# Two transformer blocks in one program: the small products of two pairs of recurrent heads and of the attention heads in common steps, between runs of 21 dense products

## The chip, the cores and the metric

One core of a Trainium2 chip runs the whole program in one launch. The metric is device time in microseconds (us), the median of several runs. A profile of one execution stands beside the times.

The engines: TensorE (PE in the profile; its weight loads are PEld) multiplies, VectorE (DVE) and ScalarE (ACT) do the elementwise work, GpSimd (POOL) a little of it, SyncE (SP) issues the weight transfers. Each engine executes its own list in order and waits where a value that it needs isn't there.

## The reference, cut to what matters

256 tokens of width 2048 (and 16 learned tokens ahead of them in the first block), float32. The first block computes, from one input projection, 16 recurrent heads (RWKV-7), 16 attention heads with a forget gate, and gates that merge the two:

```python
xn = _rms(h, n1)
z_rwkv, z_fox, z_gate = jnp.split(xn @ w_in, ...)
y_a = _rwkv7(z_rwkv + (z_prev - z_rwkv) * mu, ...)   # 16 heads of 64
y_b = _fox(z_fox, ...)                               # 16 heads of 64
merged = g_a * (y_a @ w_a) + g_b * (y_b @ w_b)
h = h + merged @ w_o
h = h + (jax.nn.silu(gate) * up) @ w_dn              # gate, up = _rms(h, n2) @ w_gu

def step(S, inp):                                    # in _rwkv7, per token
    r_t, w_t, k_t, v_t, a_t, b_t = inp               # a = -kk, b = kk * a
    sa = jnp.einsum('bhvk,bhk->bhv', S, a_t)
    S = S * w_t[:, :, None, :] + sa[..., None] * b_t[:, :, None, :] + v_t[..., None] * k_t[:, :, None, :]
    return S, jnp.einsum('bhvk,bhk->bhv', S, r_t)
```

kk is k normalised over the 64 values of a head; the heads' outputs are normalised per head, and a bonus term sum(r * k * r_k) * v is added. In _fox q and k are normalised per head and the scores carry the sums of the log forget gates. The second block has a Hyena convolution, latent attention (MLA) and a gated feed-forward with a short convolution; its filters come from a small network with two sines.

## The kernel before, in words

Activations lie feature-major, 128 features by tokens. A dense product takes a weight block of 128x128 float32 (a "k step"), split into a high part (wh, a cast on ScalarE, line 192) and a low part (wl, a subtraction on VectorE, line 193), and three matmuls for it: wh with the high part of x, wl with the high part, wh with the low part (`mm3`, lines 216 to 218). Weights come in pieces of 8 k steps, that is 24 matmuls, through three buffers each for the raw piece wr, for wh and for wl. PSUM has four tags of two buffers: d for the dense products of the heads' stage, and a, b, c for the small ones.

The stage of the heads (`phase_heads`) is 80 dense blocks of 16 k steps, in the order of `in_order`: for each of 8 pairs of recurrent heads the blocks k, v, r; for each pair of attention heads fk, fq, fv; and 32 gate blocks, which `GATES_PER_PAIR` spreads among the pairs. In between come the small products. For a recurrent pair (`rwkv_pair`) these are, one behind the other: a first headsum (sums over each head's 64 rows, `headsum`, lines 296 and 297: a product with the block matrix bo of a high part rs_r and a low part rs_q) for the norm of kk; on VectorE then a, b and the bonus term; a second headsum for that term; matrices within chunks of 64 tokens (gs, psum a); four levels of an inverse (lines 1228 and 1232); transposes; the recurrence over five chunks (psum c); and the group norm with two more headsums. `rstd` is 1/sqrt from ScalarE with a correction on VectorE (lines 313 to 322). `fox_pair` has a headsum each for k and q (`headnorm`), then scores, softmax, transposes and values for each head.

The code of a pair is written in one piece. The framework's scheduler decides by priorities (the order of the code, with weights ahead) and due times where each instruction goes on its engine; so the small products fall among the dense ones singly or in groups.

Behind the heads: the merge, w_o, the first feed-forward; then the mix (`phase_mix`), beside which `filters` works out the Hyena filters (its sines on ScalarE, L747; `transforms` loads fspec and splits it into dh and dl); `phase_out`, whose `rstd` has a "warm" argument: products without use, written by PE in the time of the norm; the convolution feed-forward; and `phase_last`, with w_down2.

Of the kernel before, what the change touches and what calls it, by code (L numbers as in the profile page):

```python
# [18 lines left out]
P = 128  # L19
# [35 lines left out]
GATES_PER_PAIR = (2, 0, 2, 3, 3, 2, 2, 2, 0)  # L55
# [96 lines left out]
class Builder:  # L152
# [60 lines left out]
    def mm3(self, out, wh, wl, xh, xl, start, stop):  # L213

        nc = self.nc
        nc.tensor.matmul(out, lhsT=wh, rhs=xh, start=start, stop=False)  # L216
        nc.tensor.matmul(out, lhsT=wl, rhs=xh, start=False, stop=False)  # L217
        nc.tensor.matmul(out, lhsT=wh, rhs=xl, start=False, stop=stop)  # L218
# [71 lines left out]
    def headsum(self, ps, w, src, n, pool=None):  # L290

        hi, lo = (self.tl(pool or self.small, [P, L if pool is None else n], t)[:, :n] for t in ("rs_r", "rs_q"))
        hi = hi.bitcast(F32R)
        lo = lo.bitcast(F32R)
        self.split(src, hi, lo)
        self.nc.tensor.matmul(ps, lhsT=w, rhs=hi, start=True, stop=False)
        self.nc.tensor.matmul(ps, lhsT=w, rhs=lo, start=False, stop=True)

# [5 lines left out]
    def rstd(self, out, ss, n, scale, eps, floor=None, pool=None, warm=None):  # L304
# [13 lines left out]
        for x in (r, q) if warm is not None else ():  # L318

            nc.tensor.matmul(warm, lhsT=self.con("ones"), rhs=x, start=True, stop=True)  # L320
# [4 lines left out]
    def run(self):  # L325
# [8 lines left out]
        self.wlo = self.pool(ctx, "wlo", 3)  # L334
        self.psum = {t: self.pool(ctx, "ps" + t, 2, PSUM) for t in "dabc"}
# [120 lines left out]
    def fox_pair(self, j):  # L456
        nc, w, w2 = self.nc, self.pfx, self.pfx2
        ident = self.con("ident")
        kn = self.headnorm(self.proj("fk", j, 0), 0, w, w2, "fk", self.col("kg"))
        qn = self.headnorm(self.proj("fq", j, NM), NM, w, w2, "fq", self.qgs)  # L460
        ps = self.proj("fv", j, 0)
        v = self.tl(w, [P, T], "fv")
        nc.vector.tensor_tensor(out=v, in0=ps, in1=self.R, op=ALU.mult)
        vt = self.tl(w2, [P, 3, P], "fvt")
# [6 lines left out]
        y = self.tl(w2, [P, S], "fy")  # L471
        for h in range(2):
            hs = slice(64 * h, 64 * h + 64)
            sel = self.oh[hs, 2 * j + h : 2 * j + h + 1].broadcast_to([64, P])
            pt = self.tl(w, [P, 5, P], "fpt")
            for b in range(2):
# [8 lines left out]
                self.softmax(sc, mx, -1.0, w2)  # L485
                ps = self.ps("b").rearrange("p (c x) -> p c x", c=4)
# [9 lines left out]
            out = self.ps("b")[:, :S]  # L496
            nc.tensor.matmul(out[hs], lhsT=vt[:, 0, hs], rhs=pt[:, 0:2], start=True, stop=False)
            nc.tensor.matmul(out[hs, 0:128], lhsT=vt[:16, 1, hs], rhs=pt[:16, 3], start=False, stop=False)
            nc.tensor.matmul(out[hs, 128:256], lhsT=vt[:, 1, hs], rhs=pt[:, 2], start=False, stop=False)
            nc.tensor.matmul(out[hs, 128:256], lhsT=vt[:16, 2, hs], rhs=pt[:16, 4], start=False, stop=True)  # L500
            nc.scalar.copy(y[hs], out[hs])
        nc.scalar.dma_start(out=self.sp_yb[j], in_=y)

    def headnorm(self, ps, t0, w, w2, tag, gain):
# [7 lines left out]
        ps = self.ps("b")[:, :n]  # L512
        self.headsum(ps, self.bo, sq, n, w)
# [3 lines left out]
        return zn  # L517
# [79 lines left out]
    def phase_mix(self, xh, xl, ys, rs):  # L597
# [3 lines left out]
        with ExitStack() as c:  # L601
# [24 lines left out]
            accq, rq, acck = (self.tl(w, [P, S], n) for n in ("rope_t", "rq", "acch"))  # L626
            cqh, cql = (self.tl(w, [P, 4, S], n, F32R) for n in ("hyh", "hyl"))
# [11 lines left out]
            self.rstd(acck, self.total(acck), S, 1.0 / 256, 1e-6)  # L639
            kvh, kvl = (self.tl(w, [P, 2, S], n, F32R) for n in ("huh", "hul"))  # L640
# [76 lines left out]
    def filters(self, c):  # L717
# [5 lines left out]
        dh, dl = (self.tl(w, [P, 1024], n, F32R) for n in ("dh", "dl"))  # L723
        cfi = self.tl(w, [P, S], "cfi")
# [7 lines left out]
        self.transforms(w, ((dh, dl, 0),))  # L732
        dh, dl = (x.rearrange("p (k f) -> p k f", k=2) for x in (dh, dl))
# [23 lines left out]
        h2 = sine(ps, self.col("f_b2"), self.col("f_f2"), "s2")  # L757
        yield
# [169 lines left out]
    def phase_last(self, pg, hh, hl, spill):  # L928
# [20 lines left out]
        for g in range(4):  # L949
            gs = slice(512 * g, 512 * g + 512)  # L950
            ps = [self.ps("a"), self.ps("d")]
            for i in range(HT // 2):
                wh, wl = (x.rearrange("p (k x) c -> p k (x c)", k=2) for x in self.weights(a["w_down2"][22 * g + i], PIECE))
# [83 lines left out]
    def phase_heads(self):  # L1037
# [5 lines left out]
        with ExitStack() as pr:  # L1043
# [39 lines left out]
            self.fox_setup(pr)  # L1083
            for j in range(9):
                if j < 8:
                    self.rwkv_pair(j, w)
                if j == 0:
                    self.forget_gates()
                if j:
                    self.fox_pair(j - 1)  # L1090
                for _ in range(GATES_PER_PAIR[j]):
                    self.gate()
            while self.ngate < 32:
                self.gate()

# [19 lines left out]
    def rwkv_pair(self, j, w):  # L1115
# [8 lines left out]
        self.lerp(self.proj("r", j, 14), self.col("mu_r", j), 14, 16, zr[:, 64:])  # L1124

# [20 lines left out]
        nc.vector.scalar_tensor_tensor(out=kk, in0=z, scalar=self.col("k_k", j), in1=kk, op0=ALU.mult, op1=ALU.mult)  # L1146
        bk = self.tl(w, [P, NC5, 2, 64], "bk")
# [13 lines left out]
        ps = self.ps("b")[:, :S]  # L1161
        self.headsum(ps, self.bo, t1[:, 64:], S)
# [6 lines left out]
        gm = self.crw("gmask").rearrange("p (x t) -> p x t", x=2)  # L1169
        for h in range(2):  # L1170
            hs = slice(64 * h, 64 * h + 64)
# [9 lines left out]

        uv = self.tl(w2, [P, NC5, P], "uv")
        v0 = self.tl(w2, [64, NC5, 64], "v0")
        bt = self.tl(w2, [P, NC5, P], "bt")
        bs = self.tl(w, [P, NC5, P], "bs")
        ed = self.tl(w2, [P, NC5], "ed")
        nc.gpsimd.tensor_copy(ed, ee[:, 0].rearrange("p (c t) -> p c t", t=64)[:, :, 63])
        for c in range(NC5 - 1):
            nc.vector.tensor_scalar(out=bs[:, c], in0=bk[:, c].rearrange("p x t -> p (x t)"),
                                    scalar1=ed[:, c : c + 1], scalar2=None, op0=ALU.mult)  # L1190
# [4 lines left out]
        for c0, n in ((0, 3), (3, 2)):  # L1195
            ps = self.ps("a").rearrange("p (c x) -> p c x", c=4)
            for c in range(n):
                nc.tensor.transpose(ps[:, c], zv[:, 64 * (c0 + c) : 64 * (c0 + c) + 128], self.con("ident"))
            nc.scalar.copy(uv[64:128, c0 : c0 + n], ps[64:128, :n])
            nc.vector.tensor_copy(v0[:, c0 : c0 + n], ps[64:128, :n, 0:64])  # L1200
# [17 lines left out]
        for lv in range(1, 5):  # L1218
# [3 lines left out]
            lm = level(lv, c0)  # L1222
            ps = pv()
# [4 lines left out]
            nc.vector.tensor_tensor(out=pp[:, c0:], in0=ps[:, c0:], in1=eye.broadcast_to([P, n, 64]), op=ALU.add)  # L1228
            ps = pv()
# [10 lines left out]
            if lv == 3:  # L1240
                nc.gpsimd.tensor_copy(xf[:, 0], xt[:, 0])
        ps = self.ps("a")[:, :P].rearrange("p (c t) -> p c t", c=4)
# [6 lines left out]
        nc.scalar.copy(y5[96:128], ps[96:128])  # L1249
# [186 lines left out]
```

## Time and profile before

| what | us |
|---|---|
| median of 3 runs (lowest, highest) | 2824.17 (2823.87, 2826.2) |
| the profiled execution | 2825.54 |
| its span | 2823.8 |
| PE busy in the span | 2798.4 |
| heads' stage, 31.4 to 785.9 | 754.5, PE busy 753.81 |
| the rest, 785.9 to the end | 2037.9, PE busy 2015.81 |
| VectorE, ScalarE busy in the heads' stage | 518.7, 411.3 |

How to read it: a row of the timeline has start and length in us, engine, line, operation, the tiles written and read, the shape of the array's use (rows*columns) and of the operands. In square brackets stands the idle time in front and what ended it. Starts of neighbours on PE lie closer than the lengths say, since matmuls are pipelined. The granted clock is 1.00 at full speed.

### The profile page before, as it was taken

How to read it: one execution, taken by the hardware profiler on the slowest of the kernel's cores; microseconds unless marked ns; L12 is line 12 of the kernel's file. 1: busy time of each engine (PE TensorE's matmuls, PEld its weight loads, DVE VectorE, ACT ScalarE, POOL GpSimd, SP SyncE). 2: the span in 40 equal slices, each digit the busy share in tenths (PEclk: the TensorE clock that was granted, in tenths of full speed). 3: DMA queues.
4: the chain of work that ended last, by engine and by line, in shares of the span. 5: the costliest groups of instructions: out<-in, count | busy, mean ns of one | idle time of the engine just before them, and what ended most of it. 6: DMA issues, size and time to landing. Idle time of an engine off the chain costs nothing.

```text
span 2823.8 us, 56202 instructions
## 1 busy us (share of the span) xinstructions
PE 2798.4 (99%) x23288; PEld 2637.9 (93%) x23288; DVE 1847.1 (65%) x2958; ACT 1346.8 (48%) x1994; POOL 143.2 (5%) x294
## 2 busy tenths in 40 slices
PE   9999999999999999999999999999999999999998
PEld 9988888888999999999999999999989999998886
DVE  8857667676566665656565556787787777775444
ACT  7545555555444554444444445444454444444443
POOL 0000000010000200000000000001100000000000
PEclk9999999999999999999999999999999999999999
DMA  7333333334576555566656666444556555556554
GB/s 246 128 110 116 102 109 116 106 105 137 184 238 211 189 188 195 194 194 194 194 195 201 202 202 216 162 148 144 189 192 193 194 194 194 194 193 230 191 191 163
DMA packets 147741, 497.13 MB, mean 176 GB/s; under 512 B 16252, under 2 KB 30941, under 8 KB 146909
## 3 DMA queue, kind: packets, MB, share of 16 engines
q1 hardware_dynamic: 128448, 458.42, 49.7%
q10 hardware_dynamic: 18396, 33.03, 3.4%
q8 instruction: 182, 2.98, 0.4%
q0 software_dynamic: 640, 2.10, 0.3%
q14 instruction: 75, 0.61, 0.1%
HBM read 478.27 MB, written 15.20 MB: 175 GB/s over the span
## 4 chain that ended last, share of the span: by engine, by line
PE 96%; DVE 2%; DMA 1%; ACT 1%; issue 0%; POOL 0%; DVEq 0%; ACTq 0%; POOLq 0%
PE psd L218 12%; PE psd L216 12%; PE psd L217 12%; PE psa L217 5%; PE psa L218 5%; PE psb L218 5%; PE psb L216 5%; PE psa L216 5%; PE psb L217 5%; PE psc L217 4%; PE psc L218 4%; PE psc L216 4%; PE psa L959 1%; PE psd L960 1%; PE psa L960 1%; PE psd L959 1%
## 5 line engine op out<-in xcount | busy, mean ns | idle before, releaser
L193 DVE TENSOR_TENSOR wl<-wr,wh 128x1024 fp32r<-128x1024 f32 (+1 forms) x872 | 1063.7, 1220 | 629.1 <-ACT wh L192 627.9
L192 ACT CAST wh<-wr 128x1024 fp32r<-128x1024 f32 (+1 forms) x872 | 909.1, 1043 | 1157.6 <-PE psd L218 337.4
L218 PE MATMUL psd<-xl,wh 128*128 128x256 f32 (+2 forms) x1280 | 370.4, 289 | 0.0
L216 PE MATMUL psd<-xh,wh 128*128 128x256 f32 (+2 forms) x1280 | 369.5, 289 | 0.0
L217 PE MATMUL psd<-xh,wl 128*128 128x256 f32 (+2 forms) x1280 | 367.9, 287 | 0.4 <-DVE wl L193 0.4
L218 PEld LDWEIGHTS psd<-xl,wh 128*128 128x128 f32 x1280 | 240.6, 188 | 7.7 <-issue 2.3
L217 PEld LDWEIGHTS psd<-xh,wl 128*128 128x128 f32 x1280 | 240.8, 188 | 6.5 <-issue 2.1
L216 PEld LDWEIGHTS psd<-xh,wh 128*128 128x128 f32 x1280 | 240.6, 188 | 6.3 <-issue 1.8
L218 PE MATMUL psd<-x3l,wh 128*128 128x256 f32 x496 | 140.7, 284 | 0.0
L216 PE MATMUL psd<-x3h,wh 128*128 128x256 f32 x496 | 140.6, 283 | 0.0
L217 PE MATMUL psd<-x3h,wl 128*128 128x256 f32 x496 | 138.9, 280 | 0.0
L216 PE MATMUL psd<-x4h,wh 128*128 128x256 f32 x368 | 100.5, 277 | 2.8 <-ACT x4h L252 2.8
L217 PE MATMUL psd<-x4h,wl 128*128 128x256 f32 x368 | 101.5, 277 | 1.1 <-DVE wl L193 1.0
L218 PE MATMUL psd<-x4l,wh 128*128 128x256 f32 x368 | 101.2, 277 | 0.0
L262 POOL TENSOR_TENSOR acc<-acc,ssq 128x256 f32<-128x256 f32 x42 | 58.4, 1391 | 817.8 <-ACT ssq L264 813.4
L217 PE MATMUL psa<-x4h,wl 128*128 128x256 f32 x352 | 97.0, 277 | 1.0 <-DVE wl L193 1.0
L218 PE MATMUL psa<-x2l,wh 128*128 128x256 f32 x352 | 97.4, 277 | 0.0
L216 PE MATMUL psa<-x2h,wh 128*128 128x256 f32 x352 | 97.4, 277 | 0.0
L218 PE MATMUL psb<-x2l,wh 128*128 128x256 f32 x352 | 97.2, 276 | 0.0
L217 PE MATMUL psb<-x2h,wl 128*128 128x256 f32 x352 | 97.2, 276 | 0.0
L216 PE MATMUL psb<-x2h,wh 128*128 128x256 f32 x352 | 97.2, 276 | 0.0
L218 PE MATMUL psc<-x2l,wh 128*128 128x256 f32 x352 | 97.2, 276 | 0.0
(673 smaller groups left out, 8390.9 us busy)
## 6 DMA issues: line engine op xcount, KB each, us to landing
wr<-w_in_dram SPq DMA_DIRECT2D x230, 512.0 KB, 3.4
wr<-w_gu_dram SPq DMA_DIRECT2D x176, 512.0 KB, 4.1
wr<-w_down_dram SPq DMA_DIRECT2D x176, 512.0 KB, 4.2
wr<-w_up_dram SPq DMA_DIRECT2D x176, 512.0 KB, 3.5
wr<-w_ab_dram SPq DMA_DIRECT2D x32, 512.0 KB, 4.2
wr<-w_o_dram SPq DMA_DIRECT2D x32, 512.0 KB, 3.4
wr<-w_out_dram SPq DMA_DIRECT2D x32, 512.0 KB, 3.6
spill_g<-acc ACTq DMA_DIRECT2D x32, 128.0 KB, 2.1
```

The costliest lines, as they stand in the source:

```text
L192: self.nc.scalar.copy(hi, src)
L193: self.nc.vector.tensor_tensor(out=lo, in0=src, in1=hi.bitcast(F32), op=ALU.subtract)
L216: nc.tensor.matmul(out, lhsT=wh, rhs=xh, start=start, stop=False)
L217: nc.tensor.matmul(out, lhsT=wl, rhs=xh, start=False, stop=False)
L218: nc.tensor.matmul(out, lhsT=wh, rhs=xl, start=False, stop=stop)
L262: nc.gpsimd.tensor_tensor(out=acc, in0=acc, in1=self.pending[id(acc)], op=ALU.add)
L959: nc.tensor.matmul(ps[b], lhsT=hh[:, k, bs], rhs=wl[:, q], start=False, stop=False)
L960: nc.tensor.matmul(ps[b], lhsT=hl[:, k, bs], rhs=wh[:, q], start=False, stop=k == HT - 1)
```

## The change: what it does

`rwkv_pair`, `headnorm`, `headsum` and the attention heads become generators ("chains") that stop at marked places (`yield`). `dense` counts its k steps. After every 7 of them (TICK, 21 matmuls) every chain that is alive goes one step on, that is, it issues what lies between two marks. The step's instructions are ordered behind the dense product before it, and the next dense product behind the step's instructions on PE. Up to two recurrent pairs and a pair of attention heads are alive at a time.

Along with that: the blocks k, v, r and their shifts are in `rwkv_inputs`; the transposes of v stand between the first two headsums; the products k-v of all five chunks are made in one group before the recurrence, which then adds them on VectorE; the values of the attention heads take psum a, and both score blocks of a head are in one step, with their transposes two steps later; `GATES_PER_PAIR` is new, and the forget gates are worked out within the first pair's gate blocks.

Outside the heads: `transforms` stands behind the second sine in `filters`; the warm products in `rstd` are six in place of two; three pads (48, 32 and 16 columns) move tiles in `phase_mix` and `filters`; the weights of w_down2 lie 48 columns further in their buffers.

```diff
-GATES_PER_PAIR = (2, 0, 2, 3, 3, 2, 2, 2, 0)
+GATES_PER_PAIR = (5, 2, 3, 2, 3, 2, 3, 5, 0)
+TICK = 7
...
     def dense(self, out, st, kt, xh, xl, tok):
         for k in range(kt):
             wh, wl = next(st)
-            self.mm3(out, wh, wl, xh[:, k, tok], xl[:, k, tok], k == 0, k == kt - 1)
+            with ExitStack() as held:
+                for i in self.hold:
+                    held.enter_context(self.tc.issue_after(i))
+                m = self.mm3(out, wh, wl, xh[:, k, tok], xl[:, k, tok], k == 0, k == kt - 1).ins
+            self.hold = []
+            self.since += 1
+            if self.chains:
+                self.hold = [m]
+                if self.since >= TICK:
+                    self.since = 0
+                    self.tick(m)
+
+    def tick(self, ins):
+        for c in list(self.chains):
+            with self.tc.issue_after(ins):
+                if next(c, self) is self:
+                    self.chains.remove(c)
+        traced = self.nc.cur_bb.bb.instructions
+        at = next(k for k in reversed(range(len(traced))) if traced[k] is ins)
+        self.hold = [i for i in traced[at:] if i.engine == ins.engine]
...
-    def headsum(self, ps, w, src, n, pool=None):
+    def headsum(self, bank, w, src, n, pool=None):
...
         self.split(src, hi, lo)
+        yield
+        ps = self.ps(bank)[:, :n]
         self.nc.tensor.matmul(ps, lhsT=w, rhs=hi, start=True, stop=False)
         self.nc.tensor.matmul(ps, lhsT=w, rhs=lo, start=False, stop=True)
+        return ps
...
-        for x in (r, q) if warm is not None else ():
+        for x in (r, r, r, q, q, q) if warm is not None else ():
...
-        self.transforms(w, ((dh, dl, 0),))
...
         h2 = sine(ps, self.col("f_b2"), self.col("f_f2"), "s2")
+        self.transforms(w, ((dh, dl, 0),))
...
+            self.tl(w, [P, 48], "apart")
...
+            self.tl(w, [P, 32], "away")
...
-                wh, wl = (... for x in self.weights(a["w_down2"][22 * g + i], PIECE))
+                wh, wl = (... for x in self.weights(a["w_down2"][22 * g + i], PIECE, off=48))
...
             for j in range(9):
                 if j < 8:
-                    self.rwkv_pair(j, w)
-                if j == 0:
-                    self.forget_gates()
+                    self.rwkv_inputs(j)
+                    self.drain(pairs[-2:-1])
+                    pairs.append(self.chain(self.rwkv_pair(j, w)))
                 if j:
-                    self.fox_pair(j - 1)
-                for _ in range(GATES_PER_PAIR[j]):
+                    self.drain(fox)
+                    fox = [self.fox_pair(j - 1)]
+                else:
+                    fox = []
+                for i in range(GATES_PER_PAIR[j]):
                     self.gate()
+                    if i == 1 and j == 0:
+                        self.forget_gates()
...
     def rwkv_pair(self, j, w):
...
-        ps = self.ps("b")[:, :L]
-        self.headsum(ps, self.bo, sq, L)
+        ps = yield from self.headsum("b", self.bo, sq, L)
         kk = self.tl(w, [P, L], "kk")
         self.rstd(kk, ps, L, 1.0, 0.0, floor=1e-24)
         nc.vector.scalar_tensor_tensor(out=kk, in0=z, ...)
+        yield
+        for c0, n in ((0, 3), (3, 2)):
+            ps = self.ps("a").rearrange("p (c x) -> p c x", c=4)
+            for c in range(n):
+                nc.tensor.transpose(ps[:, c], zv[:, ...], self.con("ident"))
...
-        ps = self.ps("b")[:, :S]
-        self.headsum(ps, self.bo, t1[:, 64:], S)
+        ps = yield from self.headsum("b", self.bo, t1[:, 64:], S)
...
+        for c in range(NC5):
+            for h, hs in enumerate(hss):
+                kat, vv = ...
+                nc.tensor.matmul(ps[hs, c], lhsT=kat, rhs=vv, start=True, stop=True)
+        kv = v0
+        nc.scalar.copy(kv, ps)
```

Where this puts instructions, at three places. New line numbers are higher: the dense matmuls are L217 to L219, the headsum L333 and L334, the splits L194 on VectorE. Names carry buffer numbers.

On PE, the first headsum of the first pair. Before, its two products stand apart, behind several hundred dense rows of the opening:

```order
L217 MATMUL psd_237_1268<-xh_6_94,wl_240_1271 128x272
L218 MATMUL psd_237_1268<-xl_7_95,wh_239_1270 128x272
L296 MATMUL psb_115_735<-rs_r_116_736,bo_67_472 128x320
L216 MATMUL psd_237_1268<-xh_6_94,wh_239_1270 128x272
L217 MATMUL psd_237_1268<-xh_6_94,wl_240_1271 128x272
...
L218 MATMUL psd_237_1268<-xl_7_95,wh_242_1300 128x272
L297 MATMUL psb_115_735<-rs_q_117_737,bo_67_472 128x320
L216 MATMUL psd_237_1268<-xh_6_94,wh_242_1300 128x272
```

After, both stand in one step, three rows behind the products of the gate of the recurrence (psb with adh and adl):

```order
L217 MATMUL psd_117_739<-xh_6_94,wh_119_741 128x256
L218 MATMUL psd_117_739<-xh_6_94,wl_120_742 128x256
L219 MATMUL psd_117_739<-xl_7_95,wh_119_741 128x256
L217 MATMUL psb_110_720<-adh_56_447,wh_107_709 128x272
L218 MATMUL psb_110_720<-adh_56_447,wl_108_710 128x272
L219 MATMUL psb_110_720<-adl_57_448,wh_107_709 128x272
L333 MATMUL psb_121_749<-rs_r_115_735,bo_67_472 128x320
L334 MATMUL psb_121_749<-rs_q_116_736,bo_67_472 128x320
L217 MATMUL psd_117_739<-xh_6_94,wh_119_741 128x256
```

The headsum moved forward on PE by some hundred dense rows.

On PE, the second headsum of the second pair (pair 1). Before, it is together with a headsum of the attention's keys (the one of 272 columns):

```order
L218 MATMUL psd_409_2045<-xl_7_95,wh_414_2077 128x272
L1232 MATMUL psa_153_850<-xt_146_828,pp_152_848 64x64 x10
L296 MATMUL psb_284_1524<-rs_r_285_1525,bo_67_472 128x256
L297 MATMUL psb_284_1524<-rs_q_286_1526,bo_67_472 128x256
L296 MATMUL psb_386_1946<-rs_r_387_1947,bo_67_472 128x272
L297 MATMUL psb_386_1946<-rs_q_388_1948,bo_67_472 128x272
L216 MATMUL psd_409_2045<-xh_6_94,wh_414_2077 128x272
```

After, products of the first pair's recurrence (psc) stand in the same step:

```order
L219 MATMUL psd_289_1693<-xl_7_95,wh_291_1695 128x256
L1371 MATMUL psc_294_1713<-st_276_1647,ar_131_797 64x64 x2
...
L1360 MATMUL psc_295_1717<-ar_131_797,st_241_1499 64x64
L333 MATMUL psb_296_1723<-rs_r_283_1672,bo_67_472 128x256
L333 MATMUL psb_305_1740<-rs_r_287_1689,bo_67_472 128x272
L334 MATMUL psb_305_1740<-rs_q_288_1690,bo_67_472 128x272
L334 MATMUL psb_296_1723<-rs_q_284_1673,bo_67_472 128x256
L217 MATMUL psd_289_1693<-xh_6_94,wh_291_1695 128x256
```

Between the pair's first headsum and this one there are 42 dense rows now.

On VectorE, the end of the work for that headsum (kk to the split rs_q of the bonus term t). Before:

```order
L1154 TENSOR_SCALAR t1_282_1514<-av_53_442,cols_1_61 128x320
L193 TENSOR_TENSOR wl_415_2078<-wr_413_2076,wh_414_2077 128x8x128
L1155 SCALAR_TENSOR_TENSOR kf_283_1515<-t1_282_1514,kz1_49_435 128x320
L509 TENSOR_TENSOR fq_400_2024<-psd_393_1963,R_3_85 128x256
L193 TENSOR_TENSOR wl_447_2196<-wr_445_2194,wh_446_2195 128x8x128
L1156 TENSOR_TENSOR bk_280_1512<-kf_283_1515,ep_271_1490 128x5x64
L1160 SCALAR_TENSOR_TENSOR t1_282_1514<-zr1_51_437,cols_1_61,kf_283_1515 128x256
L1228 TENSOR_TENSOR pp_152_848<-psa_151_837,con_2_62 128x320
L1268 COPY rhs_178_978<-psc_177_975 128x64
L1189 TENSOR_SCALAR bs_299_1564<-bk_280_1512,ed_300_1565 128x128 x4
L193 TENSOR_TENSOR rs_q_286_1526<-t1_282_1514,rs_r_285_1525 128x256
```

After:

```order
L194 TENSOR_TENSOR wl_321_1811<-wr_319_1809,wh_320_1810 128x8x128
L1235 TENSOR_TENSOR t1_281_1662<-kk_266_1605,av_53_442 128x320
L1240 SCALAR_TENSOR_TENSOR ar_280_1661<-kk_266_1605,ee_255_1562 128x5x64
L1372 TENSOR_TENSOR rhs_293_1712<-psc_294_1713,v0_127_763 128x64
L194 TENSOR_TENSOR rs_q_288_1690<-fsq_286_1687,rs_r_287_1689 128x272
L1236 TENSOR_TENSOR bk_279_1660<-t1_281_1662,ep_256_1563 128x5x64
L1237 TENSOR_SCALAR t1_281_1662<-av_53_442,cols_1_61 128x320
L1238 SCALAR_TENSOR_TENSOR kf_282_1663<-t1_281_1662,kz1_49_435 128x320
L1239 TENSOR_TENSOR bk_279_1660<-kf_282_1663,ep_256_1563 128x5x64
L1243 SCALAR_TENSOR_TENSOR t1_281_1662<-zr1_51_437,cols_1_61,kf_282_1663 128x256
L1258 TENSOR_SCALAR bs_303_1733<-bk_279_1660,ed_304_1734 128x128 x4
L194 TENSOR_TENSOR rs_q_284_1673<-t1_281_1662,rs_r_283_1672 128x256
```

The same rows of the pair stand there with fewer others between them, among those fewer weight splits.

More of the change, by code (lines that the diff above doesn't have):

```diff
@@ L234, in dense, with chain, drain @@
             wh, wl = next(st)
-            self.mm3(out, wh, wl, xh[:, k, tok], xl[:, k, tok], k == 0, k == kt - 1)
+            with ExitStack() as held:
[17 more added lines that the diff above has]
+        self.hold = [i for i in traced[at:] if i.engine == ins.engine]
+    def chain(self, c):
+        next(c)
+        self.chains.append(c)
+        return c
+    def drain(self, chains):
+        for c in chains:
+            for _ in c:
+                pass
+            if c in self.chains:
+                self.chains.remove(c)
     def group(self, out, st, kt, xh, xl, toks, bring):
@@ L463, in fox_pair, with fox_heads @@
         nc.vector.tensor_tensor(out=v, in0=ps, in1=self.R, op=ALU.mult)
+        return self.chain(self.fox_heads(j, *n, v))
+    def fox_heads(self, j, kn, qn, v):
+        nc, w, w2 = self.nc, self.pfx, self.pfx2
+        ident = self.con("ident")
+        yield
         vt = self.tl(w2, [P, 3, P], "fvt")
@@ L1222, in rwkv_pair @@
             lm = level(lv, c0)
+            yield
             ps = pv()
```

147 lines of the change are left out of this document (89 added, 58 removed).

## The prediction

> **What bounds the kernel now.** I read the head of the page first, then its chain of waits, then windows by stage.
>
> ```profile
> span 2823.8 us, 56202 instructions
> PE 2798.4 (99%) x23288; PEld 2637.9 (93%) x23288; DVE 1847.1 (65%) x2958; ACT 1346.8 (48%) x1994; POOL 143.2 (5%) x294
> PE 96%; DVE 2%; DMA 1%; ACT 1%; issue 0%; POOL 0%; DVEq 0%; ACTq 0%; POOLq 0%
> ```
>
> TensorE (PE) is busy 99% of the span, and 96% of the chain that ended last is PE. So time can come only from PE rows that take less, and it is lost wherever PE is made to wait. The stage of the heads, which the change rewrites, and the rest:
>
> ```profile
> 31.40:785.90 754.50, 753.81 (x6901) 665.54 (x6900) 518.69 (x1117) 411.28 (x756) 57.80 (x82) 1.00 0.39 127
> 785.90:2823.80 2037.90, 2015.81 (x16193) 1946.83 (x16192) 1305.23 (x1807) 912.21 (x1202) 84.44 (x200) 1.00 0.59 192
> ```
>
> Columns: stretch, length, then busy time (instructions) of PE, PEld, DVE (VectorE), ACT (ScalarE), POOL, then granted clock, DMA share, GB/s. In the heads PE works 753.81 of 754.50 us at full clock, VectorE 519, ScalarE 411. The chain through the heads' small products is never what PE waits for; PE's whole list of waits in that stretch is two rows:
>
> ```profile
> PE psd L217 <- DVE wl L193: 0.4, 1, 0.4
> PE psa L1232 <- DVE pp L1228: 0.2, 1, 0.2
> ```
>
> What can be saved there is therefore in how PE's rows follow each other:
>
> ```profile
> 569.99 0.29 PE L216 MATMUL psd<-xh,wh 128*128 128x272 f32 x1
> 570.12 0.28 PE L217 MATMUL psd<-xh,wl 128*128 128x272 f32 x1
> 570.24 0.29 PE L218 MATMUL psd<-xl,wh 128*128 128x272 f32 x1
> 570.46 0.33 PE L1286 MATMUL psc<-gs,uv 128*64 128x64 f32 x2
> 570.71 0.33 PE L1287 MATMUL psc<-ar,st 64*64 64x64 f32 x2
> 570.97 0.39 PE L216 MATMUL psd<-xh,wh 128*128 128x272 f32 x1
> 571.20 0.29 PE L217 MATMUL psd<-xh,wl 128*128 128x272 f32 x1
> 571.32 0.29 PE L218 MATMUL psd<-xl,wh 128*128 128x272 f32 x1
> ```
>
> Read the distances between starts (the durations overlap). Dense to dense is 0.12-0.13 us. From the last dense row to a product of another array shape (128*64) it is 0.22; from the first dense row after the small ones to the second it is 0.23. So a departure from the dense shape costs about 0.10 on the row before it, a return about 0.10 on its first row.
>
> **1. Longer dense runs: -20.4 us.** By the two orders, dense rows that are followed directly by a product of another shape fall from 201 to 114, and returns from 209 to 135; the multiplications are the same. 87 x 0.095 + 74 x 0.105 (medians over the stage of the two distances above, less the plain step) = 16.0 us. The products among themselves also stand in fewer mixed rows. To price that, each row of the stage was given the median distance of its line, size and neighbour shapes: before's order comes to 750.9 us, 3.4 short of what was measured, after's to 730.5. The difference, 20.4, is taken; the ends are 16.0 and 24 (20.4 and the 3.4 that the pricing leaves unexplained).
>
> [...]
>
> **2. The second headsum of each pair: a wait that isn't there now, +36 us for seven pairs.** Between the first headsum and the second lie, on VectorE, the norm of the keys, all of a, b, the bonus term and its split. Before, 87 to 114 dense rows lie between the two on PE; now two steps do, 42 rows. In the pair in which before needs least time for it (VectorE rows, and PE's first row of the second headsum):
>
> ```profile
> 447.31 0.49 DVE L315 TENSOR_SCALAR rs_v<-psb 128x320 f32<-128x320 f32 x1
> 449.38 0.49 DVE L321 SCALAR_TENSOR_TENSOR rs_q<-rs_q,rs_v 128x320 f32<-128x320 f32 x1 [0.84 <-ACT rs_q L317]
> 450.32 1.23 DVE L193 TENSOR_TENSOR wl<-wr,wh 128x1024 fp32r<-128x1024 f32 x1
> 453.43 1.22 DVE L193 TENSOR_TENSOR wl<-wr,wh 128x1024 fp32r<-128x1024 f32 x1
> 457.62 1.23 DVE L193 TENSOR_TENSOR wl<-wr,wh 128x1024 fp32r<-128x1024 f32 x1 [0.39 <-ACT wh L192]
> 459.54 0.42 DVE L193 TENSOR_TENSOR rs_q<-t,rs_r 128x256 fp32r<-128x256 f32 x1
> 461.74 0.40 PE L296 MATMUL psb<-rs_r,bo 128*128 128x256 f32 x2
> ```
>
> From 447.31 to 459.96 the path takes 12.65 us, with three weight splits (wl) of 1.14 from start to start in it. In the new order the VectorE rows of pair 1 from rs_v to that rs_q are 22, two of them wl: 2.28 us for these and 8.0 for the others by their durations in the trace, 10.3 in all, with no wait counted. With the 0.84 for ScalarE's rsqrt and square, and a weight cast ahead of them, it is 11.5 to 13.4. PE meanwhile has 42 x 0.12 = 5.0, the transposes of v with about 1, and 1.0 to 1.4 of other chains: 7.0 to 7.4. PE executes in order and its next dense row is held until the step's products are issued, so it stands. By VectorE's rows alone the seven stalls are 3.0 to 6.3 us, 31.7 in sum (the lower end); with ScalarE's part about 5.2 each, 36; at most 40. The same sums over before's order give no stall at all, as its trace shows. Nothing behind the step can hide this: all dense rows stand behind it on PE, and weights are already ahead.
>
> **3. The first pair: +12 us.** Its first headsum stands behind 147 dense rows now, at 50.7 us by the trace's steps, where before it came at 64.18:
>
> ```profile
> 53.73 0.28 PE L218 MATMUL psb<-adl,wh 128*128 128x272 f32 x1
> 64.18 0.31 PE L296 MATMUL psb<-rs_r,bo 128*128 128x320 f32 x1
> 50.80 0.43 DVE L1033 TENSOR_TENSOR lerp_d<-p 128x256 f32<-128x256 f32 x1
> 53.89 0.82 DVE L1133 TENSOR_TENSOR_SCAN cc<-crw,sg 128x320 f32<-128x320 f32 x1
> 62.11 0.48 DVE L193 TENSOR_TENSOR rs_q<-sq,rs_r 128x320 fp32r<-128x320 f32 x1
> ```
>
> VectorE reaches 50.80 in step with PE, and the split that PE needs ends at 62.59. Between lie 11.8 us, of which three of its four weight splits (3.4) now fall behind it: ready at about 59.5, so PE stands 8.8. Its second headsum has 42 rows again, but fewer products of others beside it, and costs 2.9: 11.7 in all, 8.7 by VectorE's rows without the second (lower end), 12 at most. Stalls together: 48, between 40 and 52.
>
> **4. The clock after a stall: +13 us.** Behind the heads, the trace shows what a PE wait can bring:
>
> ```profile
> 818.00:821.40 3.40, 1.52 (x13) 1.00 0.72 258
> 821.40:828.20 6.80, 6.69 (x28) 0.50 0.50 145
> 818.68 1.05 ACT L192 CAST dh<-fspec 128x1024 fp32r<-128x1024 f32 x1 [3.94 <-DMA fspec<-chy_dram]
> 821.51 1.11 PE L755 MATMUL psb<-s1x,fw 64*64 64x256 f32 x2 [1.99 <-ACT s1x L747]
> 2079.20 0.61 PE L320 MATMUL psc<-rs_q,con 128*128 128x256 f32 x2
> 2079.85 0.43 DVE L321 SCALAR_TENSOR_TENSOR rs_q<-rs_q,rs_v 128x256 f32<-128x256 f32 x1 [0.78 <-PE psc L320]
> 2082.58 0.39 PE L216 MATMUL psd<-x4h,wh 128*128 128x256 f32 x1 [2.77 <-ACT x4h L252]
> ```
>
> (The first two rows: PE busy, granted clock.) An idle of 1.99 us is followed by 6.8 us at half clock, 3.4 us lost; one of 2.77 before the last product stage is not followed by a drop. Eight new stalls of 3 to 9 us: between 0 and 8 x 3.4 = 27 us; I take half, 13, since one of the two shown dropped.
>
> **5. The filters' spectrum: -5.3 us.** The rows at 818.68 and 821.51 are one story: PE waits for a sine on ScalarE, which stood behind the cast dh, 3.94 us for its DMA:
>
> ```profile
> fspec<-chy_dram ACTq DMA_DIRECT2D x1, 512.0 KB, 12.5
> ```
>
> 12.5 us to landing, issued last of five. In the new order ScalarE issues it first of them, 14 rows earlier, and casts dh ahead of the others; the sine keeps its place. The idle of 1.99 and the 3.4 behind it go. If the sine is late for another reason, nothing is gained. A loss needs that DMA to be slow alone too: with two weight casts between issue and cast, up to 12.5 of wait against three buffered pieces (8.4 us of PE), 4. Bounds +4 and -5.3.
>
> **6. Four more warm products: +1.7 us.** In phase_out, the multiplier at 2079.85 writes over rs_q, and waited 0.78 for the products that read it. Each of the two shown takes about 0.4 (0.61 and 0.70 with overlap); 4 x 0.43 = 1.7 goes on this chain. Bounds 0, if ScalarE's later work were the limit, and 2.4.
>
> **7. Addresses: -1 us.** w_down2's weights lie 48 columns further, and three pads move tiles:
>
> ```profile
> L960 PE MATMUL psd<-wh,hl 128*128 128x512 f32 x176 | 69.3, 394 | 0.0
> L958 PE MATMUL psa<-wh,hh 128*128 128x512 f32 x176 | 68.4, 388 | 0.0
> L218 PE MATMUL psd<-x3l,wh 128*128 128x256 f32 x496 | 140.7, 284 | 0.0
> L216 PE MATMUL psd<-x4h,wh 128*128 128x256 f32 x368 | 100.5, 277 | 2.8 <-ACT x4h L252 2.8
> ```
>
> The same product takes 388 or 394 ns by its tiles, so addresses count for some ns: 6 x 352 = 2.1 us, either way; I take -1. In the stage of the mix the products of x3 take 284 where those of x4 take 277: 7 x 496 = 3.5 us for each third of it that a pad could mend or spoil. I take nothing there, and up to 7 either way for the range.
>
> At nothing: ten table loads fewer on ScalarE (which is busy 55% of the heads; nothing on PE waits for it there now), the moved transposes, the one group for all kv, the fox scores taken together, and the new order of gates. Their cover is the 42 dense rows of two steps, and it holds for each but the headsums; the norms of fox may add under 1 us each.
>
> **Sum.** 2825.5 (the profiled execution) - 20.4 + 36 + 12 + 13 - 5.3 + 1.7 - 1 = 2861.5. That execution is 1.4 above the median of the three runs, so 2860.
>
> **Rivals.**
> - *The clock holds.* Stalls of 3 to 6 us are too short, or lie badly for it: without the 13, 2847. For it: the 2.77 us that did nothing.
> - *The clock drops at all eight.* 27 in place of 13: 2874. For it: 1.99 us sufficed once, and each new stall is longer.
> - *The runs of 21 bring nothing*, because the steps' own mixtures of shapes cost what the dense rows save: without the 20.4 the stalls stand bare, at 2880. Against it: the priced sum meets before's stage within 3.4 us.
> - *Faster.* The second headsum's data come in time, because VectorE runs its chain ahead and the two wl fall behind it. VectorE's work without wl is 8.0, with 0.84 of wait 8.8, against 7.2 on PE: 1.6 per pair. Then 7 x 1.6 + 9 replaces 48 + 13, and it is 2820; without any wait, 2799. The point from which it decides is 25 us of stalls and drops in all, 3 for each pair. Against it: the order of VectorE, where the wl stand in between.
>
> [...]
>
> **How the numbers follow.** Half of the drops 0.35, none 0.24, all 0.14; runs bring nothing 0.05; short stalls (2820 to 2830) 0.08; none or nearly (2799) 0.14. A measurement of this kernel can tell 0.2%, 5.6 us. Faster by more than that: the last, and a part of the short stalls: 0.17; within: 0.06; slower: 0.77. Predicted is the likeliest case, 2860. From 2816 to 2884 lie all but the faster cases and the tail of the two highest; the likeliest alone is 2850 to 2872.
>
> **What would show it.** Step 1: dense steps that sum to about 487 us in the heads, not 503. Steps 2 and 3: rows of PE waiting in psb at the headsum's lines (L333, L334) for VectorE's rs_q or ScalarE's rs_r, 3 to 6 us each, and some 9 at 51 us. Step 4: clock 0.5 in the window behind each. Step 5: no idle at the first filter product, and full clock after it. Step 6: a wait of about 2.5 us for the last of the warm products. The forecast is wrong if psb at the headsum shows waits below 3 us, or if other products of the steps wait, which I cost at nothing.

## The result, and the profile after

The changed kernel takes 2868.96 us (median of 4 runs, 2866.73 to 2870.83) against 2825.18 us before (4 runs): a ratio of 1.0153, 95% interval 1.0139 to 1.0167. It is slower by 43.8 us; 2860 was forecast, in a range of 2816 to 2884. (Of the five runs of e5 below one, the profiled one, took 4622 us at a granted clock of 0.554; it is left out, so e5 has times and no trace.) The head of the changed kernel's page, the engines of the chain that ended last, and the heads' stage and the rest in windows (the profiled execution took 2868.31 us):

```profile
span 2866.5 us, 56208 instructions
PE 2793.8 (97%) x23296; PEld 2647.1 (92%) x23296; DVE 1850.1 (65%) x2950; ACT 1338.5 (47%) x1992; POOL 140.2 (5%) x294
PE 92%; DVE 3%; DMA 2%; ACT 2%; issue 1%; POOL 0%; DVEq 0%; ACTq 0%; POOLq 0%
31.30:838.70 807.40, 755.56 (x6900) 678.44 (x6899) 524.62 (x1111) 404.67 (x755) 54.24 (x82) 0.96 0.36 119
838.70:2866.50 2027.80, 2009.32 (x16202) 1943.11 (x16201) 1303.53 (x1807) 911.67 (x1202) 84.96 (x200) 1.00 0.59 193
```

The heads went from 754.5 to 807.4 us, the rest from 2037.9 to 2027.8. PE is busy 755.56 us in the heads, hardly more than before, but idle for 51.8 where it was idle for 0.7, and the mean granted clock of the stage is 0.96 in place of 1.00. PE's waits in the heads, in full:

```profile
PE psb L333 <- ACT rs_r L193: 43.7, 10, 6.4
PE psb L334 <- DVE rs_q L194: 4.0, 7, 1.7
PE psb L217 <- ACT sg L1204: 2.2, 1, 2.2
PE psc L334 <- DVE rs_q L194: 0.9, 1, 0.9
PE psc L1382 <- DVE uv L1354: 0.6, 1, 0.6
PE psd L218 <- DVE wl L194: 0.2, 1, 0.2
```

(Total, times, longest.) Two rows before, 0.6 us; now 51.6 us, 48 of them at the psb headsums. One such wait in the timeline, that of pair 2's second headsum, with VectorE's rows in the same stretch and the one ScalarE row that releases PE:

```profile
223.00 0.57 PE L1382 MATMUL psc<-uv,bt 128*64 128x64 f32 x4
223.11 0.48 DVE L360 SCALAR_TENSOR_TENSOR kk<-rs_q,rs_r 128x320 f32<-128x320 f32 x1
223.62 0.44 DVE L569 TENSOR_TENSOR fk<-psd,R 128x272 f32<-128x272 f32 x1
...
225.03 1.22 DVE L194 TENSOR_TENSOR wl<-wr,wh 128x1024 fp32r<-128x1024 f32 x1
226.17 0.48 DVE L1240 SCALAR_TENSOR_TENSOR ar<-kk,ee 128x320 f32<-128x320 f32 x1
226.57 0.48 DVE L1236 TENSOR_TENSOR bk<-t,ep 128x320 f32<-128x320 f32 x1
226.97 0.43 DVE L194 TENSOR_TENSOR rs_q<-fsq,rs_r 128x272 fp32r<-128x272 f32 x1
...
228.67 0.48 DVE L1243 SCALAR_TENSOR_TENSOR t<-zr,cols,kf 128x256 f32<-128x256 f32 x1
229.06 0.87 DVE L1258 TENSOR_SCALAR bs<-bk,ed 128x128 f32<-128x128 f32 x4
229.18 0.40 ACT L193 CAST rs_r<-t 128x256 fp32r<-128x256 f32 x1 [4.21 <-DVE t L1243]
229.64 0.81 PE L333 MATMUL psb<-rs_r,bo 128*128 128x256 f32 x2 [6.07 <-ACT rs_r L193]
```

Read it from the end. PE waits 6.07 us for ScalarE's rs_r; ScalarE had waited 4.21 for VectorE's t; VectorE works through from 223 to 229 without a gap. The list of waits names ScalarE, but VectorE is what is late: its row of some 20 instructions is longer than 42 dense matmuls and a step. And behind such a wait (stretch, length, PE busy, granted clock):

```profile
229.60:234.60 5.00, 4.96 (x23) 0.50 0.00 0
325.70:329.70 4.00, 3.90 (x18) 0.50 0.01 2
```

PE works at half clock. In windows of 1 us over the whole stage there are 11 such places, and (1 - clock) x PE busy sums to 23.7 us. So the stage's +52.9 us are: 51.0 more of waiting, 23.7 of half clock, and -21.8 for the rows themselves (807.4 - 51.6 - 23.7 = 732.1 against 754.5 - 0.6 = 753.9).

### The profile page after: what moved, and what is told of

The parts are those of the page before. It is cut to its first block, busy times and chain, and to the rows that moved or that the text cites. A ratio compares the mean times of both kernels' runs of the same rounds, so it can differ in the third digit from the quotient of the medians.

```text
span 2866.5 us, 56208 instructions
## 1 busy us (share of the span) xinstructions
PE 2793.8 (97%) x23296; PEld 2647.1 (92%) x23296; DVE 1850.1 (65%) x2950; ACT 1338.5 (47%) x1992; POOL 140.2 (5%) x294
## 4 chain that ended last, share of the span: by engine, by line
PE 92%; DVE 3%; DMA 2%; ACT 2%; issue 1%; POOL 0%; DVEq 0%; ACTq 0%; POOLq 0%
PE psd L217 12%; PE psd L219 11%; PE psd L218 11%; PE psa L218 4%; PE psb L217 4%; PE psa L219 4%; PE psb L219 4%; PE psb L218 4%; PE psa L217 4%; PE psc L219 4%; PE psc L218 4%; PE psc L217 4%; PE psa L1020 1%; PE psa L1021 1%; PE psa L1022 1%; PE psd L1021 1%
## 5 line engine op out<-in xcount | busy, mean ns | idle before, releaser
L194 DVE TENSOR_TENSOR wl<-wr,wh 128x1024 fp32r<-128x1024 f32 x872 | 1063.0, 1219 | 659.5 <-ACT wh L193 658.7
L193 ACT CAST wh<-wr 128x1024 fp32r<-128x1024 f32 x872 | 908.7, 1042 | 1181.2 <-PE psd L219 366.7
L217 PE MATMUL psd<-xh,wh 128*128 128x256 f32 (+2 forms) x1280 | 384.9, 301 | 0.0
L219 PE MATMUL psd<-xl,wh 128*128 128x256 f32 (+2 forms) x1280 | 369.5, 289 | 0.0
L217 PEld LDWEIGHTS psd<-xh,wh 128*128 128x128 f32 x1280 | 249.5, 195 | 13.2 <-issue 6.0
L218 PEld LDWEIGHTS psd<-xh,wl 128*128 128x128 f32 x1280 | 249.6, 195 | 0.4 <-DVE wl L194 0.4
L219 PEld LDWEIGHTS psd<-xl,wh 128*128 128x128 f32 x1280 | 248.8, 194 | 0.0
L217 PE MATMUL psd<-x3h,wh 128*128 128x256 f32 x496 | 140.3, 283 | 1.4 <-DVE yy L690 1.4
L219 PE MATMUL psd<-x3l,wh 128*128 128x256 f32 x496 | 140.3, 283 | 0.0
L217 PE MATMUL psd<-x4h,wh 128*128 128x256 f32 x368 | 100.8, 278 | 2.8 <-ACT x4h L287 2.8
L219 PE MATMUL psd<-x4l,wh 128*128 128x256 f32 x368 | 101.1, 277 | 0.0
L219 PE MATMUL psa<-x2l,wh 128*128 128x256 f32 x352 | 97.4, 277 | 0.0
L217 PE MATMUL psa<-x2h,wh 128*128 128x256 f32 x352 | 97.4, 277 | 0.0
L219 PE MATMUL psb<-x2l,wh 128*128 128x256 f32 x352 | 97.2, 276 | 0.0
L217 PE MATMUL psb<-x2h,wh 128*128 128x256 f32 x352 | 97.2, 276 | 0.0
L219 PE MATMUL psc<-x2l,wh 128*128 128x256 f32 x352 | 97.2, 276 | 0.0
```

Of the source, the lines that this page charges most:

```text
L193: self.nc.scalar.copy(hi, src)
L194: self.nc.vector.tensor_tensor(out=lo, in0=src, in1=hi.bitcast(F32), op=ALU.subtract)
L219: return nc.tensor.matmul(out, lhsT=wh, rhs=xl, start=False, stop=stop)
```

## The experiments

Theory: the dense runs do save about 20 us, and waits at the headsums, with the half clock behind them, cost 75. Rivals: the chains have no room, so that a wait removed turns up elsewhere; the half clock has a cause of its own; the gain doesn't come from the shapes; the 10 us outside the heads belong to the heads' new order.

**e1, room before the second headsum.** `headsum` can stand more than one step behind its split:

```diff
         self.split(src, hi, lo)
-        yield
+        for _ in range(1 + gap):
+            yield
...
-        ps = yield from self.headsum("b", self.bo, sq, L)
+        ps = yield from self.headsum("b", self.bo, sq, L, gap=4 if j == 0 else 0)
...
-        ps = yield from self.headsum("b", self.bo, t1[:, 64:], S)
+        ps = yield from self.headsum("b", self.bo, t1[:, 64:], S, gap=2)
```

> The changed kernel with two more steps between the split of a pair's bonus term and its second headsum (84 dense rows in place of 42), and four more ahead of the first pair's first headsum. Theory: the 44 us that the change costs are about 51 us of PE waiting at the headsums and 22 us of half clock behind these waits, against 20 us less for changes of array shape and 10 us less outside the heads. Then the waits at the psb headsums fall from 48 us to under 5, the granted clock of the whole goes from 0.986 to 0.997 or more, the heads' stage takes about 735 us and the kernel about 2800 (2793 to 2808). Rival: the chain has no room for more steps, so that the waits only move (into the recurrence, the group norm or the last drain): 2825 to 2860, with other rows in the list of waits.

2838.97 us, ratio to before 1.0043 (1.0028 to 1.0058): 30 us better than the changed kernel, not 69, and in the range of the rival, though the waits stay at the headsums and not where it put them. The two rows of the psb headsums in the list of waits, and four of PE's rows:

```profile
PE psb L335 <- DVE rs_q L194: 13.5, 15, 2.1
PE psb L334 <- ACT rs_r L193: 7.7, 9, 2.0
74.93 0.38 PE L335 MATMUL psb<-rs_q,bo 128*128 128x256 f32 x1 [1.10 <-DVE rs_q L194]
132.52 0.58 PE L335 MATMUL psb<-rs_q,bo 128*128 128x256 f32 x1 [1.27 <-DVE rs_q L194]
306.71 0.60 PE L335 MATMUL psb<-rs_q,bo 128*128 128x272 f32 x1 [1.32 <-DVE rs_q L194]
389.64 0.60 PE L335 MATMUL psb<-rs_q,bo 128*128 128x272 f32 x1 [2.11 <-DVE rs_q L194]
```

Of 48 us of waits 21 stay. Those of 272 columns are the headsums of the attention's keys. Their split stands in the same row of VectorE's work: in the timeline above it starts at 226.97 and takes 0.43, while PE stood from 223.57 on. In the changed kernel they stand in the same step as the second headsum, whose wait is longer, to 229.64. So one wait had hidden another. And half clock follows 8 of the short waits, 15.1 us in sum:

```profile
75.00:78.00 3.00, 3.00 (x26) 1.00 0.64 187
132.60:135.60 3.00, 3.00 (x13) 0.50 0.57 180
306.80:309.80 3.00, 3.00 (x14) 0.50 0.50 169
```

The stage is 777.1 us: 26 of waiting, 15 of half clock, and 736 for the rows, 18 less than before.

**e2, one step more** (`gap=1` at the second headsum alone).

> The changed kernel with one more step (63 dense rows) before the second headsum, nothing for the first pair's first. An added step is about 3 us of PE work, so the waits of pairs 1 to 7 (3.0 to 6.3 us) should fall to 0 to 3.2 us each, 14 in sum in place of 37. It shows how long an idle has to be for the clock to fall. If it takes an idle of over 3.4 us, only the first pair's drop is left and the time is about 2869 - 23 - 18 = 2828. If idles of 1.5 to 3 us suffice, three or four of the drops stay: about 2838.

2847.02 us in one run. 2828 is missed for e1's reason: the waits at the psb headsums fell from 48 to 32 only, and ten half-clock places stay, 18.5 us. The first reading (it takes over 3.4 us) is out: in the changed kernel half clock stands behind the wait of 2.80 us too, from 504.33 to 507.74. The second (1.5 to 3 us suffice) is nearer, but e1's waits of 1.27 and 1.32 us lie under it.

**e3 and e8, the wait filled.** PE gets products without use right ahead of the headsum:

```diff
+        full = self.ps(bank)
+        ps = full[:, :n]
+        for _ in range(fill):
+            self.nc.tensor.matmul(full[:, 384:448], lhsT=self.con("ident"), rhs=self.con("ones")[:, :64], start=True, stop=True)
         self.nc.tensor.matmul(ps, lhsT=w, rhs=hi, start=True, stop=False)
```

> The changed kernel, with products without use (128x128 by 64 columns, into unused columns of the headsum's own psum tile, 15 to 56 of them by the length of the wait) issued on PE just ahead of the second headsum of each pair and of the first pair's first: PE works where it waited, and the headsum comes no sooner. Theory (the clock falls because PE is idle): the half-clock windows behind eight of the eleven waits go, the time falls by 16 to 20 us to about 2850. Rival (the half clock has another cause, or is a consequence of something in the heads' order): 2868, clock as before. If a product takes longer than the 0.11 us assumed, up to 10 us more in both cases.

2902.24 us: too many products, as the size of one had been mistaken.

```profile
L335 PE MATMUL psb<-con 128*128 128x64 f32 x756 | 97.1, 294 | 0.0
```

There are two records to each of the 378, 95 us in all from start to start: 0.23 us each, and 0.4 each for the 56 in front of the first pair's first headsum. The time tells nothing on the clock. Its places of half clock in the heads fell from 11 to 2, but one of the two is long:

```profile
54.60:78.45 23.85, 23.85 (x113) 0.50 0.08 28
```

The clock fell behind the 2.21 us wait at the first pair's gates, and PE then wrote those 56 products without a gap, from 53.15 to 75.8, at half clock; it came back within 3 us of the dense products behind them. In front of the second headsums, where the clock stood at full, the products kept it there. So in e3 these products held the clock where it was full, and didn't raise it where it was half. Again, sized:

> As e3, for pairs 1 to 7 alone, with as many products without use as fit in each wait. In e3 one took 0.257 us and not 0.11, so that 378 of them took 97 us where 48 us of waiting were to be filled; here 10 to 24 by the pair, 133 in all, 34 us for 35 us of waits. Nothing comes sooner on any other engine. Theory (the half clock follows from PE being idle): the drops behind the seven waits go, 16 us, and the time is 2853 (2848 to 2858). Rival (it does not): 2866 to 2872, as the changed kernel.

2857.37 us, 11.6 less than the changed kernel. Half clock in the heads fell from 23.7 us to 7.7 (4 places, the first pair's among them, which isn't filled); the stage from 807.4 to 795.2. No headsum's data came sooner by the products, and still the time fell by most of the clock's share; the products take 33 us where the waits fell by 29, which is the other 4. So filling PE's idle did away with most of the half clock behind it: 13 of the 16 us lie in the seven filled pairs, where two places of 1.7 us stay, and the rest at places that were not filled.

**e4, the edits outside the heads alone**, made on the kernel before: the spectrum's place, the warm products, the pads, w_down2's 48 columns (the diff of these is in the section on the change).

> The kernel before with only the edits outside the heads: the filters' spectrum behind the second sine, six warm products for two, the three pads, w_down2 by 48 columns. Theory: the 10 us that the rest of the program is shorter come from these edits alone: 2815 (2812 to 2818), of which about 7.5 before the first feed-forward's first product (the filters), 2.4 in the last stage, +1.3 at the warm products. Rival: they come with the heads' new order (where memory lies, what is loaded ahead): 2822 to 2828.

2818.38 us, ratio 0.9971 (0.9959 to 0.9982). That is 8.7 us less, 0.4 above the range: most of the 10.1 us that the rest of the changed kernel is shorter comes from these edits (8.5 by the stages below), and 1.6 stay open. By stages of the profiled executions, in us:

| stage | before | changed | e4 |
|---|---|---|---|
| merge of the branches, with the filters' start | 114.3 | 108.9 | 110.1 |
| w_o | 95.9 | 93.7 | 93.7 |
| mix, to the first product of x4 | 363.3 | 364.5 | 363.1 |
| convolution feed-forward's first products | 484.5 | 483.2 | 483.2 |
| last stage | 256.7 | 254.3 | 256.1 |

**e5 and e6, what a change of shape costs.** On e1's kernel, one product more in the middle of each dense run, adding zeros to the dense tile; it takes 64x64 of the array in one kernel (shown) and 128x128 in the other:

```diff
+                elif self.since == 3 and k < kt - 1:
+                    with self.tc.issue_after(m):
+                        d = self.nc.tensor.matmul(out[:64, :64], lhsT=self.con("ident")[:64, :64], rhs=self.zmid[:64], start=False, stop=False).ins
+                    self.hold = [m, d]
```

> The kernel of e1 (two more steps), and in the middle of each run of 21 dense matmuls one more product that adds zeros to the dense psum tile: 64x64 by 64 columns, another array shape than the dense ones; 158 of them. Theory (a departure from the dense shape costs 0.095 us and a return 0.105, besides the product): 158 x (0.1 to 0.2 for the product itself + 0.20) = 47 to 63 us over e1, so 2886 to 2902, and 32 us (28 to 36) over the kernel with the same product in full shape. Rival (the runs' length and the shape don't matter, what the change gains in the heads comes from elsewhere): the two kernels within 5 us of each other.

> The same 158 products of zeros with all 128x128 of the array, by 64 columns: no change of shape. Theory: they cost themselves alone, 16 to 32 us over e1's 2839, so 2855 to 2871, and 28 to 36 us less than with 64x64. Rival: the same time as with 64x64, within 5 us.

2895.9 us (median of four; ratio 1.0243, 1.0227 to 1.0258) with 64x64, 2860.01 (1.0122, 1.0108 to 1.0136) with 128x128, run on the same chip. The difference is 35.9 us for 158 products, 0.23 us for a departure and a return, where the prediction had 0.200. In it is also whatever a 64x64 product itself takes more or less than one of 128x128, and what the two kernels differ by in waits and clock; these were not told apart.

**e7, room for the attention's norms too**: `gap=1` in `headnorm`, and `gap=3` at the second headsum of pairs 1 to 7.

> The kernel of e1 with one more step for the headsums of the attention's q and k too, and a third for the second headsum of pairs 1 to 7. e1 left 25 us of PE waits in the heads, nearly all at psb headsums for VectorE's rs_q, 1 to 2 us each, and 15 us of half clock behind them. Theory: these waits fall to under 8 us (the first pair's two of 1.2 and 1.1 and the last group norm's two stay), and the clock drops to one or two places (3 us); heads 777 - 19 - 12 = 746, time 2839 - 31 = 2808 (2803 to 2815). Rival: VectorE is what is short of time in these steps, so waits of 1 us turn up at the next products of the chains (matrices, scores): 2825 to 2840.

2811.60 us, ratio 0.9943 (0.9930 to 0.9955): faster than the kernel before, by 14.2 us, of which 9.0 lie in the heads (745.5 us against 754.5). Its stage of the heads, and PE's waits there:

```profile
31.20:776.70 745.50, 728.84 (x6900) 654.40 (x6900) 513.50 (x1107) 395.52 (x746) 55.85 (x82) 1.00 0.39 127
PE psb L335 <- DVE rs_q L194: 6.8, 6, 1.8
PE psa L1228 <- ACT xtf L1346: 4.4, 2, 3.4
PE psb L334 <- ACT rs_r L193: 3.0, 2, 2.0
PE psa L1228 <- ACT xtf L1319: 1.0, 1, 1.0
PE psc L1328 <- DVE rs_v L352: 0.9, 1, 0.9
PE psc L1383 <- DVE uv L1355: 0.4, 1, 0.4
```

PE is busy 728.84 us, 25 less than before, and waits 16.5, of which 9.8 are at headsums (under 8 was expected) and 6.7 at other places, as the rival had named: VectorE and ScalarE are nearly late at several steps. The theory's 746 for the stage is met, and 2811.60 lies in its range.

**e9, the first pair alone** (`gap=4 if j == 0` at the first headsum, nothing else).

> The changed kernel with four more steps ahead of the first headsum of the first pair alone (231 dense rows ahead of it in place of 147). It takes away the first pair's waits (2.2, 6.4 and 1.7 us) and the half clock behind them (3.7 us of loss), less about 1.5 of wait that e1 still showed there. Theory: 2869 - 12 = 2857 (2853 to 2862), the other pairs unchanged. Rival (the first pair's later end pushes work into the drain ahead of the third pair): 2864 or more.

2864.32 us: 4.6 less, not 12. The first pair's two headsums:

```profile
62.03 0.41 PE L334 MATMUL psb<-rs_r,bo 128*128 128x320 f32 x1 [1.23 <-ACT rs_r L193]
72.71 0.58 PE L334 MATMUL psb<-rs_r,bo 128*128 128x256 f32 x1 [4.23 <-ACT rs_r L193]
```

The first wait fell from 6.40 to 1.23, and the second rose from 1.68 to 4.23: with the first headsum later, the second is still 42 rows behind it, and the long wait no longer gives VectorE time. The rival's number is met, by another mechanism than it named: the third pair's wait (pair 2) rose only from 6.07 to 6.83.

## Why the prediction was right, and where it was not

**What bounds.** PE's rows were the bound, and the loss came as PE waiting at the headsums, for VectorE's row, with half clock behind. That was right: with more room for VectorE the kernel is 12 us slower than before in e1, and 14 faster in e7, where it was 44 slower.

**Step 1, longer runs, -20.4.** The rows themselves came out 21.8 lower (what is left when waits and half clock are taken off), 18 in e1, 28 in e7 (745.5 - 16.5 - 3.4); why these three lie 10 us apart was not tried. The rival in which the runs bring nothing is out. e5 against e6 puts the change of shape at 0.23 us for both directions, near the 0.200 read from the timeline; at that size the 87 departures and 74 returns are 18 us, by estimate.

**Step 2, second headsums, +36.** The seven waits at L333 were 4.23, 6.07, 5.31, 5.94, 2.80, 4.27 and 5.98 us: 34.6 in sum. Adding up VectorE's row in its new order, with durations from the old trace, gave 31.7 as the least and 36 with ScalarE. One of the seven, 2.80, is under the 3 us that the prediction named as a sign against itself.

**Step 3, the first pair, +12.** 2.2 + 6.4 + 1.7 = 10.3; of these 2.2 stand at the first pair's gates and not at its headsum. So PE came to the first headsum at 53.69 and not at 50.7, its data at 60.09 and not at 59.5 (the prediction's own figures, 62.59 - 3.4, give 59.2), and the stall of 8.8 is 6.40. The other 6.7 us of waits in the heads (attention norms, group norms) had been put at nothing, or under 1 us each.

**Step 4, the clock, +13.** This is the term that was mis-sized. All eight long idles were followed by half clock, some 19 us, and three places with shorter ones (1.68, 1.01 and 0.31 us) too, 5: 23.7 in all. The eight cost about 2.3 each and not 3.4, as part of each stretch of half clock lies in the wait itself. Half of the drops was chosen because one of two idles in the trace had dropped; the rival with all of them (27, 2874) had their number right, and 2868.96 lies between the two.

**Step 5, the filters, -5.3.** The merge is 5.4 us shorter after and 4.2 in e4; in the changed kernel PE has no wait and no half clock in that stretch any more.

**Step 6, warm products, +1.7.** The rows that answer to those at 2079, with six records of each kind where there were two, the wait of VectorE for them and the clock behind:

```profile
2123.33 1.56 PE L358 MATMUL psc<-rs_r,con 128*128 128x256 f32 x6 [0.56 <-ACT rs_r L350]
2124.73 1.46 PE L358 MATMUL psc<-rs_q,con 128*128 128x256 f32 x6
2126.28 0.42 DVE L359 SCALAR_TENSOR_TENSOR rs_q<-rs_q,rs_v 128x256 f32<-128x256 f32 x1 [2.55 <-PE psc L358]
2129.01 0.55 PE L217 MATMUL psd<-x4h,wh 128*128 128x256 f32 x1 [2.82 <-ACT x4h L287]
2129.10:2132.40 3.30, 3.30 (x16) 0.50 0.16 68
```

From the first warm product to the first x4 row it is 5.68 us, where it was 3.92: +1.8. VectorE waits 2.55 us for the last of them, where it waited 0.78, as the prediction said. The idle behind them is as long as it was, 2.82 and 2.77, but now half clock follows it, as it didn't before.

**Step 7, addresses, -1.** It was more: w_down2's products came to one duration, and w_o takes 2.2 less, with no wait of PE in it in either kernel.

```profile
L1022 PE MATMUL psd<-wh,hl 128*128 128x512 f32 x176 | 68.5, 389 | 0.0
L1020 PE MATMUL psa<-wh,hh 128*128 128x512 f32 x176 | 68.6, 390 | 0.0
```

394 became 389, and the last stage is 2.4 shorter (0.6 in e4, where PE waits 1.1 us more). Which pad gave w_o its 2.2 us was not tried. The 1.3 us of the convolution feed-forward are another thing: before, PE waited twice about 1 us for wl in it, and after it doesn't (2.2 in all); its rows take 0.9 less, and the half clock above takes 1.7 back.

That the sum came within 9 us is in part luck, as the errors of its terms lay against each other: the clock cost 10.7 more than in the sum and the waits 3.0 more, while the rest of the program gained 5.5 more and the runs 1.4. The rival "faster" named a point from which it decides, 25 us of waits and half clock in the heads. The kernels fit it: e1, with 41, is slower than the kernel before, and e7, with 20, is faster.

## What to carry to other kernels

Where an engine that is the bound is given a fixed place for each product, add up the other engine's row between the value's first input and its use, in the new order with the durations of the old trace, and hold it against the bound's own work in between: that named the eight long waits here, and the seven second headsums within 2 us in sum (36 against 34.6). Grouping products by array shape was worth some 0.2 us here for each departure and return saved, so a wait of one microsecond eats what five of them bring. When one wait is taken away, look for what waited beneath it (e1), and for what the wait had given time to (e9).

## What was not expected of the hardware

The clock fell after shorter idles than those that the prediction weighed (2 to 9 us). In e1, waits of 1.27 and 1.32 us are each followed by over 3 us at half clock, one of 1.10 us by none; a wait of 1.72 us in the changed kernel, at 424 us, by none either. So half clock followed 1.27 us once and not 1.72 us another time: the length of the wait alone doesn't tell.

The traces show what goes with a drop. In all ten of them (all but e5's) a stretch of half clock within the kernel lasts 3.41 us or a whole multiple of it (6.83, 10.24, once 23.89), and within a run all stretches start on one grid of that step: in the changed kernel those at 227.85, 323.42 and 408.76 us lie 28 and 25 steps of 3.413 apart. Of the steps of this grid that lie at full clock in the heads' stage of these traces, PE was busy less than half of the time in 35, and half clock follows 33 of them; it follows 18 of the 53 with PE busy for half to three quarters, and 2 of the 2121 above that.

In those last two steps PE was hardly idle or not at all. One, in the changed kernel at 149.3 us, has a single wait of 0.31 us in 3.41. The other is in e4, where PE has no wait at all; it is full of the heads' small products (stretch, length, PE busy, granted clock):

```profile
613.25:616.65 3.40, 3.40 (x24) 1.00 0.36 112
616.70:620.05 3.35, 3.35 (x17) 0.50 0.32 116
```

The same products in the kernel before, 0.15 us earlier, are followed by full clock (1.00 from 616.65 to 620.05). Most rows of the step in the changed kernel are such small products too; why half clock follows these two is not shown.

In the heads of the changed kernel and of e6 to e9 a drop cost 1.5 to 3.2 us (e3's long one 12); e1's wait of 1.27 us lost 1.5 us behind it in the 3.00 us shown at half clock, more than itself. Products without use in the wait prevented the drop in five of the seven filled pairs (e8).
